# Layer 2's output projection as two blocks of seven products, with partial results and sums moved by accumulating transfers

## Chip, cores and metric

One core of one Trainium2 chip runs the whole program. The metric is the device time of one execution in microseconds; the kernel before has a median of 912.91 us over 3 runs (912.36 to 913.66). All data are float32.

## What is computed

Two layers over a 512 x 1024 sequence. Layer 1 is differential attention, layer 2 a spatial-gating MLP; each adds its result to the stream, and a final RMS norm ends the program. The change touches the end of layer 2:

```python
def spatial_gating_branch(h, w_in, v_gain, w_s, b_s):
    proj = h @ w_in                          # 512x1024 @ 1024x6144
    u = proj[..., :BRANCH]                   # BRANCH = 2048
    v = rms_norm(proj[..., BRANCH:2 * BRANCH], v_gain)
    gate = proj[..., 2 * BRANCH:]
    ...
    y = jnp.einsum('gts,bcsgd->bctgd', w, v) + b_s.T[:, :, None]
    return u * y * jax.nn.silu(gate)

x = x + y @ sgu_w_out[j]                     # 512x2048 @ 2048x1024
return rms_norm(x, final_norm)
```

## The kernel before

**Products in three terms.** A float32 product is made of three matmuls: each operand is split into a high part (ScalarE, ACT, a cast) and a low part (VectorE, DVE, the difference), and hi·hi, hi·lo and lo·hi are added in PSUM.

**Blocks of seven products.** Layer 2's input projection is cut into six blocks (n = 0 to 5), each 512 x 1024 by 1024 x 1024. `Quads` does a block by the Strassen-Winograd scheme: seven products of quarters instead of eight. It keeps the four quarters a, b, c, d of the weights in SBUF, loads each with two 512 KB transfers of SyncE's queue (SP, L355), and turns them step by step into the seven right operands: b-=d and a=b-a by DVE subtractions (L360, two of 128x1024 each), c+=a and a+=d by transfers of GpSimd's queue (POOL, L365) that add 1 MB within SBUF. Before each product a quarter is split, two pieces of 128x1024 by ACT (L373) and DVE (L374). `work(j)` yields these pieces for product j; `beside` sets one piece between two groups of matmuls, two products ahead of use. The left operands are quarters of the normed input and their sums s1 to s4, made once, since all six blocks have the same left side. A result quarter that several products share is held (`hold`, an ACT copy from PSUM to a tile "raw") and added later by DVE (`times`).

`product_n` (24 matmuls of 128x512) is used for blocks 0 and 1 (the values v), `product_t` (48 of 128x256) for blocks 2 to 5 (gates and u, transposed). `times` multiplies them into yT, 128 x 16 x 512, so that after block 3 the first half of y (yT 0 to 7) is complete, after block 5 the second.

**The end.** `out_half` runs twice, once for each half of the 1024 output columns: four chunks of y and weights, each split (ACT L267 and L129, DVE L268 and L130), 192 matmuls of 128x512 (L273 to L275) into four PSUM banks. After each half DVE adds the banks to the stream xr (L413), ACT squares it (L206) for the norm; after the second, `emit` forms the root by a chain of small DVE operations (L180 to L187), scales (ACT L1058, DVE L1059) and stores (SP L1061).

The engines issue in program order. A wait blocks everything behind it on the same engine. A scheduler orders the instructions of each engine from the order in which the program writes them.

Of the kernel before, what the change touches and what calls it, by code (L numbers as in the profile page):

```python
# [2 lines left out]

# [1 line left out]

# [45 lines left out]
def build(ctx, tc, x, rel_bias, attn_norm, w_in, lq1, lk1, lq2, lk2, subln, w_out,  # L51
# [14 lines left out]
    def bank(name):  # L66
        return psum.tile([P, S], F32, tag="ps", name=name)
# [5 lines left out]
    def wide_src(w, c, n0):  # L73
        return w[0, c * S:(c + 1) * S, n0:n0 + S].rearrange("(k p) n -> p k n", p=P), [4, S]
# [126 lines left out]
    def square(r, b, m=None):  # L201

        sl = slice(0, D) if m is None else slice(m * S, (m + 1) * S)
        c = 0 if m is None else m
        drop = yT[:, 10:12, :].rearrange("p k n -> p (k n)") if m is None else junk
        nc.scalar.activation(drop, xr[:, b, sl], AF.Square, accum_out=sq[r][b][:, c:c + 1])  # L206
        if c == 0:
            hv[r][b] = const.tile([P, 1], F32, name=f"hv{r}_{b}")

    def row_scale(r, b, halves):  # L210

        rs = small.tile([P, 1], F32, name="rs")
        if halves:
            nc.vector.scalar_tensor_tensor(hv[r][b], sq[r][b][:, 1:2], -0.5 / D, hv[r][b], ALU.mult, ALU.add)
        else:
            half_mean(r, b)
        newton(rs, hv[r][b], 1)
        return rs

    def half_mean(r, b):  # L220
        nc.vector.tensor_scalar(hv[r][b], sq[r][b][:, 0:1], -0.5 / D, -0.5 * EPS, ALU.mult, ALU.add)

    hi_last, hT_last, xs_last = [None], [None], [None]

# [102 lines left out]
    def temp():  # L327
        return wraw.tile([P, 2, S], F32, tag="raw", name="raw")
# [474 lines left out]
    quads = Quads(qp, [columns_of(sgu_w_in, n0) for n0 in columns])  # L803
# [49 lines left out]


    wst = sp.tile([P, KB, P], F32, name="wst")
    bs_bc = sp.tile([P, KB // 2 * P], F32, name="bs_bc")

    def spread_bias(m):
        src = sgu_b_s.rearrange("o g t -> o (g t)")[:, m * KB // 2 * P:(m + 1) * KB // 2 * P]
# [45 lines left out]
            nc.vector.tensor_tensor(v, of_bank(ps[i]), v, ALU.add)  # L905
            total(v, acc)

    i0 += 8
    assert i0 == sgu_at
    late = []  # L910
    for n in range(BR // D):
        for i in range(7):
# [86 lines left out]
            nc.vector.tensor_tensor(y, v.rearrange("p (j n) -> p j n", n=H), y, ALU.mult)  # L999

    VB = BR // D
    for m in range(2):
        for gates in (True, False):
            n = VB + 2 * m + (not gates)
            final = m == 1 and not gates
            t1 = temp()
            if final:
                t4, t2 = temp(), temp()
            for i in range(7):
                work = quads.work(7 * n + i + 2)  # L1010
                if final and i == 5:
                    limit[0] = len(chunks)
                    load(i0)
                if final and i > 4:
                    work = (split(i0, 2 * (i - 5) + h) for h in range(2))
                beside(product_t(py if i in (1, 3, 6) else px, sides[i], quads.forms[n, i], i in (0, 1, 3)), work)
                if m == 0 and gates and i in (2, 3):
                    for g in range(4 * i - 8, 4 * i - 4):
                        mix(g)
                    if i == 3:  # L1020
                        spread_bias(1)
                if m == 0 and not gates and i > 2:
                    mix(5 + i)
                if m == 1 and gates and i < 4:
                    mix(12 + i)
                if i == 0:
                    hold(t1, px)
                if i == (2 if m == 0 and gates else 1):
                    times(gates, m, 0, 0, py, t1)
                if i == 2:  # L1030
                    t2 = t2 if final else temp()
                    hold(t2, px)
                if i == 4:
                    t4 = t4 if final else temp()
# [9 lines left out]
    yps = tc.tile_pool(name="yp2", bufs=2)
    yp = yps.__enter__()
    fin = yp.tile([P, D], F32, name="fin", bufs=1)
    nc.scalar.dma_start(fin, final_norm.rearrange("(o d) -> o d", o=1).broadcast_to([P, D]))
    acc = [bank(f"acc{b}") for b in range(NB)]
# [3 lines left out]
    ov = out[0].rearrange("(b p) d -> p b d", p=P)
    acc = [bank(f"acc{b}") for b in range(NB)]
    last = residual(2, 1, acc)

    def emit(b):
        rs = row_scale(2, b, True)
        nc.scalar.activation(xr[:, b, 0:S], xr[:, b, 0:S], AF.Copy, scale=rs)  # L1058
        nc.vector.scalar_tensor_tensor(xr[:, b, S:D], xr[:, b, S:D], rs, fin[:, S:D], ALU.mult, ALU.mult)  # L1059
        for m in range(2):  # L1060
            nc.sync.dma_start(ov[:, b, m * S:(m + 1) * S], xr[:, b, m * S:(m + 1) * S])  # L1061

    def finish(b):
        add = last(b)
        if b < NB - 2:
            emit(b)
        elif b == NB - 1:
            emit(b - 1)
            with tc.issue_after(add.ins):
                emit(b)  # L1070
# [25 lines left out]
```

## Time and profile before

| | |
|---|---|
| median of 3 runs | 912.91 us |
| profiled execution, its own time | 909.98 us |
| its span, first to last instruction | 908.2 us |
| PE (TensorE matmul) busy | 885.3 us, 97% |
| DVE busy | 645.3 us, 71% |
| ACT busy | 476.9 us, 53% |
| granted TensorE clock | 0.997 of full speed |

The span is the part of the time that the engines' instructions cover. Busy time is a sum over all stages; what an engine is worth at the end of the program is read from the stretches of the end. In the profile a row "L374 DVE lo<-quarter,hi" is line 374 of the kernel, on DVE, writing the tile lo from quarter and hi; "[7.38 <-DMA quarter<-quarter]" behind a row says that its engine sat idle for 7.38 us before it and that a transfer ended that.

### The profile page before, as it was taken

What the parts mean: (1) busy time and instruction counts of PE and PEld (TensorE: products, weight loads), DVE (VectorE), ACT (ScalarE), POOL (GpSimd) and SP (SyncE); (2) the same over time, 40 slices, a digit from 0 to 9 for tenths busy, and PEclk for the clock granted to TensorE, in tenths of its full rate; (3) what the DMA queues carried; (4) which work ended last, traced back from release to release, by engine and by line L of the source; (5) the groups of instructions that cost most, each with busy time, mean ns of one, the idle gap of its engine ahead of it and who ended that gap; (6) DMA issues with size and microseconds to landing.
All of it is one profiled execution on the core that took longest, in us unless ns stands there. A gap on an engine that the chain in (4) does not pass through costs nothing.

```text
span 908.2 us, 14110 instructions
## 1 busy us (share of the span) xinstructions
PE 885.3 (97%) x5393; PEld 774.6 (85%) x5393; DVE 645.3 (71%) x1399; ACT 476.9 (53%) x1015; POOL 34.4 (4%) x52
## 2 busy tenths in 40 slices
PE   7999999999999999999999999998999999999996
PEld 5878999988888888888788887787999999998884
DVE  6945665447787788688886839857795878685634
ACT  7634555446565565566664526736453444454532
POOL 0000100000000000000000002000100000000000
PEclk9999999999999999999999999999999999999998
DMA  8637755373222332321312615554656464534202
GB/s 286 234 90 210 206 192 105 116 245 95 78 90 83 103 90 83 103 89 40 105 47 82 243 29 131 188 128 151 139 163 139 141 139 140 117 134 149 86 4 93
DMA packets 55828, 115.48 MB, mean 127 GB/s; under 512 B 3965, under 2 KB 20398, under 8 KB 52432
## 3 DMA queue, kind: packets, MB, share of 16 engines
q1 hardware_dynamic: 49120, 79.70, 26.5%
q0 software_dynamic: 5584, 33.56, 15.5%
q10 hardware_dynamic: 1056, 1.32, 0.4%
q8 instruction: 42, 0.69, 0.3%
q14 instruction: 26, 0.21, 0.1%
HBM read 89.36 MB, written 6.33 MB: 105 GB/s over the span
## 4 chain that ended last, share of the span: by engine, by line
PE 82%; DVE 10%; DMA 3%; ACT 3%; issue 1%; SPq 0%; ACTq 0%; DVEq 0%; POOLq 0%
PE px L319 15%; PE py L319 11%; PE psqk L254 6%; PE psqk L256 6%; PE psqk L255 6%; PE acc L273 5%; PE acc L275 5%; PE acc L274 5%; PE psv L480 5%; PE po L732 3%; PE pss L694 3%; DMA quarter<-quarter 2%; PE pa L721 2%; DVE lo L374 2%; PE psy L981 2%; PE px L307 1%
## 5 line engine op out<-in xcount | busy, mean ns | idle before, releaser
L374 DVE TENSOR_TENSOR lo<-quarter,hi 128x1024 fp32r<-128x1024 f32 x126 | 152.8, 1236 | 86.0 <-ACT hi L373 85.6
L373 ACT CAST hi<-quarter 128x1024 fp32r<-128x1024 f32 x126 | 128.9, 1047 | 125.7 <-DMA quarter<-quarter 45.7
L130 DVE TENSOR_TENSOR lo<-raw,hi 128x512 fp32r<-128x512 f32 x144 | 93.5, 687 | 39.4 <-ACT hi L129 39.3
L129 ACT CAST hi<-raw 128x512 fp32r<-128x512 f32 x144 | 81.8, 620 | 54.9 <-PE psqk L255 24.7
L254 PE MATMUL psqk<-hT,hi 128*128 128x512 f32 x256 | 101.7, 397 | 0.0
L256 PE MATMUL psqk<-hT,lo 128*128 128x512 f32 x256 | 99.9, 390 | 0.0
L255 PE MATMUL psqk<-hT,hi 128*128 128x512 f32 x256 | 99.9, 390 | 0.0
L707 ACT ACTIVATE e<-e,nm 128x384 f32<-128x384 f32 (+3 forms) x128 | 70.8, 554 | 47.7 <-DVE nm L704 47.3
L319 PE MATMUL py<-hT,hi 128*128 128x256 f32 x512 | 93.0, 284 | 0.0
L273 PE MATMUL acc<-hi,hT 128*128 128x512 f32 x224 | 88.2, 394 | 0.5 <-DVE on L666 0.5
L274 PE MATMUL acc<-lo,hT 128*128 128x512 f32 x224 | 87.3, 390 | 0.0
L275 PE MATMUL acc<-hi,hT 128*128 128x512 f32 x224 | 87.0, 390 | 0.0
L319 PEld LDWEIGHTS py<-hT,hi 128*128 128x128 f32 x512 | 79.8, 192 | 0.0
L319 PE MATMUL py<-hT,lo 128*128 128x256 f32 x256 | 72.5, 283 | 0.0
L704 DVE CUSTOM_DVE_ANT_0 e<-pss,bias 128x384 f32<-128x384 f32 (+3 forms) x128 | 57.3, 484 | 4.1 <-PE pss L694 3.9
L254 PEld LDWEIGHTS psqk<-hT,hi 128*128 128x128 f32 x256 | 48.1, 188 | 12.9 <-issue 2.6
L268 DVE TENSOR_TENSOR hT<-yT,hT 128x512 fp32r<-128x512 f32 x56 | 37.0, 690 | 29.8 <-PE acc L274 17.4
L256 PEld LDWEIGHTS psqk<-hT,lo 128*128 128x128 f32 x256 | 48.1, 188 | 10.1
L255 PEld LDWEIGHTS psqk<-hT,hi 128*128 128x128 f32 x256 | 48.1, 188 | 9.4
L267 ACT CAST hT<-yT 128x512 fp32r<-128x512 f32 x56 | 33.5, 621 | 41.1 <-PE acc L274 35.2
L360 DVE TENSOR_TENSOR quarter<-quarter 128x1024 f32<-128x1024 f32 x36 | 43.3, 1222 | 11.5 <-DMA quarter<-in_sgu_w_in 10.8
L273 PEld LDWEIGHTS acc<-hi,hT 128*128 128x128 f32 x224 | 42.1, 188 | 10.5 <-issue 1.6
(218 smaller groups left out, 2026.6 us busy)
## 6 DMA issues: line engine op xcount, KB each, us to landing
quarter<-in_sgu_w_in SPq DMA_DIRECT2D x48, 512.0 KB, 5.4
raw<-in_attn_w_in SPq DMA_DIRECT2D x38, 512.0 KB, 4.6
quarter<-quarter POOLq DMA_DIRECT2D x18, 1024.0 KB, 7.5
quarter<-in_attn_w_in SPq DMA_DIRECT2D x24, 512.0 KB, 4.8
raw<-in_attn_w_out SPq DMA_DIRECT2D x16, 512.0 KB, 4.4
raw<-in_sgu_w_out SPq DMA_DIRECT2D x16, 512.0 KB, 4.3
vd<-yT POOLq DMA_DIRECT2D x4, 1024.0 KB, 6.0
v<-vd POOLq DMA_DIRECT2D x4, 1024.0 KB, 5.1
```

The costliest lines, as they stand in the source:

```text
L129: nc.scalar.copy(hi[:, sl], raw)
L130: nc.vector.tensor_tensor(lo[:, sl], raw, hi[:, sl].bitcast(F32), ALU.subtract)
L254: nc.tensor.matmul(ps, lhsT=w.hi[:, k, cs], rhs=hT[0][:, k, :], start=(k == 0), stop=False)
L255: nc.tensor.matmul(ps, lhsT=w.hi[:, k, cs], rhs=hT[1][:, k, :], start=False, stop=False)
L256: nc.tensor.matmul(ps, lhsT=w.lo[:, k, cs], rhs=hT[0][:, k, :], start=False, stop=(k == KD - 1))
L273: nc.tensor.matmul(acc[b], lhsT=yh[:, j, bs], rhs=w.hi[:, j, :], start=(k == 0), stop=False)
L274: nc.tensor.matmul(acc[b], lhsT=yh[:, j, bs], rhs=w.lo[:, j, :], start=False, stop=False)
L275: nc.tensor.matmul(acc[b], lhsT=yl[:, j, bs], rhs=w.hi[:, j, :], start=False, stop=(k == KB - 1))
L319: nc.tensor.matmul(ps[f // 2][:, f % 2 * H:(f % 2 + 1) * H], lhsT=w[x][:, k, f * P:(f + 1) * P], rhs=a[y][:, k, :], start=clear, stop=(k = ...
L373: nc.scalar.copy(hi[:, sl], raw[:, sl])
L374: nc.vector.tensor_tensor(lo[:, sl], raw[:, sl], hi[:, sl].bitcast(F32), ALU.subtract)
L707: nc.scalar.activation(e[f][:, cs], e[f][:, cs], AF.Exp, scale=-1.0, bias=nm[:, col], accum_out=l[:, col])
```

## The change

The output projection becomes two more blocks of `Quads` (n = 6 and 7, kb = 0 and 1): the upper 1024 rows of the weights with yT 0 to 7, the lower 1024 with yT 8 to 15, each seven times `product_n`.

- The left operands are now quarters of y. Per block `left` makes s3 = y21 - y11 (DVE, L1017), y21 += y22 (transfer of POOL's queue, 512 KB, L1018), s2 = y11 - y21 (DVE, L1020), y12 += s2 (transfer, L1021), and splits seven operands (ACT L297, DVE L298, 128x1024 each). For block 6 that stands beside the products of block 5, for block 7 beside those of block 6.
- Of the results, each of products 0, 2 and 4 of a block is held by ACT (L331) and added to xr by a transfer of POOL's queue (`put_onto`, L1082, 512 KB, six in all); those of products 1, 3, 5 and 6 are added by DVE from PSUM (`onto`, L1078).
- Sixteen loads of 512 KB bring the weights by SP as quarters (L354) in place of sixteen as chunks.
- The final norm's scale of one column half and the squares are set beside the products of block 7 (`first_half`), the rest in `emit(b, m)`: rows 0 and 1 end after product 5, rows 2 and 3 after product 6.
- `fin` and `bs_bc` share one buffer, and `fin` is loaded at the end of block 5.

The core of the diff:

```diff
+    def rows_of(w, kb):
+        def of(name):
+            r, c = divmod("abcd".index(name), 2)
+            return wide_src(w, 2 * kb + r, c * S)[0]
+        return of
+
+    blocks = [columns_of(sgu_w_in, n0) for n0 in columns] + [rows_of(sgu_w_out, kb) for kb in range(2)]
+    quads = Quads(qp, blocks)
...
+    def left(kb, i):
+        y11, y12, y21, y22 = (quarter_of(kb, q, half) for half in range(2) for q in range(2))
+        if i == "s3":
+            s3[0] = temp().rearrange("p f n -> p (f n)").rearrange("p (k n) -> p k n", n=H)
+            nc.vector.tensor_tensor(s3[0], y21, y11, ALU.subtract)
+            nc.gpsimd.dma_start(y21, y22, accum_op=ALU.add)
+        elif i == "s2":
+            nc.vector.tensor_tensor(y11, y11, y21, ALU.subtract)
+            nc.gpsimd.dma_start(y12, y11, accum_op=ALU.add)
+        else:
+            part(*sides[i], (y11, y12, y11, s3[0], y21, y12, y22)[i])
+        yield
+    def left_work(kb, i):
+        for j in ([], [0], ["s3"], [1], [3, "s2"], [2], [4])[i]:
+            yield from left(kb, j)
+    def left_rest(kb, i):
+        for j in ([], [5], [6], [], [], [], [])[i]:
+            yield from left(kb, j)
...
                 work = quads.work(7 * n + i + 2)
-                if final and i == 5:
-                    limit[0] = len(chunks)
-                    load(i0)
-                if final and i > 4:
-                    work = (split(i0, 2 * (i - 5) + h) for h in range(2))
+                if n == OUT - 1:
+                    work = chain(work, left_work(0, i))
...
+    def onto(c, half, ps):
+        ms = slice(c * S, (c + 1) * S)
+        return [nc.vector.tensor_tensor(xr[:, b, ms], ps[b % 2], xr[:, b, ms], ALU.add)
+                for b in (2 * half, 2 * half + 1)]
+    def put_onto(c, half, t):
+        nc.gpsimd.dma_start(xr[:, 2 * half:2 * half + 2, c * S:(c + 1) * S], t, accum_op=ALU.add)
...
+    for kb in range(2):
+        n = OUT + kb
+        for i in range(7):
+            work = chain(quads.work(7 * n + i + 2), left_rest(kb, i), left_work(1, i) if kb == 0 else ())
+            beside(product_n(py if i in (1, 3, 6) else px, sides[i], quads.forms[n, i], i in (0, 1, 3)), work)
+            if i in (0, 2, 4):
+                t = temp()
+                hold(t, px)
+            if i == 1:
+                onto(0, 0, py)
+                put_onto(0, 0, t)
+            if i == 2:
+                put_onto(0, 1, t)
+            if i == 3:
+                onto(1, 1, py)
+            if i == 4:
+                put_onto(1, 1, t)
+                if kb:
+                    first_half(0, 0)
+            if i == 5:
+                onto(1, 0, px)
+                if kb:
+                    for b in range(2):
+                        emit(b, 1)
+                    first_half(1, 1)
+            if i == 6:
+                adds = onto(0, 1, py)
+                if kb:
+                    emit(2, 0)
+                    with tc.issue_after(adds[1].ins):
+                        emit(3, 0)
...
-    run(out_half(i0, 0, hT_store, range(4), acc, residual(2, 0, acc)))
...
-    run(out_half(i0 + 4, 1, hT_store, range(4), acc, finish))
```

**POOL, the last rows of its queue.** The name quarter is a quarter of the weights, yT is y, raw a held result, xr the stream. Before:

```order
L860 DMA bs_bc<-in_sgu_b_s 128x1024
L365 DMA quarter<-quarter 128x2048 x6
L1092 UNCONDITIONAL_BRANCH
```

and after the change:

```order
L866 DMA bs_bc<-in_sgu_b_s 128x1024
L364 DMA quarter<-quarter 128x2048 x6
L1018 DMA yT<-yT 128x4x256
L1021 DMA yT<-yT 128x4x256
L364 DMA quarter<-quarter 128x2048 x2
L1082 DMA xr<-raw 128x2x512
L1018 DMA yT<-yT 128x4x256
L1082 DMA xr<-raw 128x2x512
L1021 DMA yT<-yT 128x4x256
L1082 DMA xr<-raw 128x2x512
```

Behind block 5's two weight sums (the last two of the x6), which ended this queue, there now come 4 sums of y, 4 weight sums and 6 result sums (two weight sums and three result sums follow the rows shown).

**DVE, the middle of the output projection.** Before, near the end of its first half:

```order
L268 TENSOR_TENSOR hT_104<-yT,hT_103 128x512 x4
L130 TENSOR_TENSOR lo<-raw,hi 128x512 x3
L413 TENSOR_TENSOR xr<-acc_8041,xr 128x512
L130 TENSOR_TENSOR lo<-raw,hi 128x512
L221 TENSOR_SCALAR hv_0_8289<-sq_0_114 128x1
```

and after the change, beside block 6 (lo and hi are the parts of a weight quarter, hT parts of a y quarter, py a result):

```order
L1078 TENSOR_TENSOR xr<-py,xr 128x512 x2
L298 TENSOR_TENSOR hT_104<-yT,hT_103 128x4x256
L373 TENSOR_TENSOR lo<-quarter,hi 128x1024 x2
L1017 TENSOR_TENSOR raw<-yT 128x1024
L298 TENSOR_TENSOR hT_104<-yT,hT_103 128x4x256
L373 TENSOR_TENSOR lo<-quarter,hi 128x1024 x2
L1078 TENSOR_TENSOR xr<-py,xr 128x512
L1020 TENSOR_TENSOR yT<-yT 128x4x256
L1078 TENSOR_TENSOR xr<-py,xr 128x512
L298 TENSOR_TENSOR hT_104<-raw,hT_103 128x4x256
```

Splits of 128x512, which were ready long ahead of use, gave way to pieces of 128x1024 with the y differences among them; L1020 stands in DVE's row behind the transfer of L1018, which stands behind L1017, which stands behind the split of the quarter that the transfer a+=d has just summed.

## Rows read from the trace of the kernel before

**Rows 1.** Page, part 1: busy us (share of the span) and instructions.

```profile
PE 885.3 (97%) x5393; PEld 774.6 (85%) x5393; DVE 645.3 (71%) x1399; ACT 476.9 (53%) x1015; POOL 34.4 (4%) x52
```

**Rows 2.** Busy time by stretches: block 5, first part, rest and tail of the output projection.

```profile
core 0: us, PE busy (x) PEld busy (x) DVE busy (x) ACT busy (x) POOL busy (x), PEclk, DMA share, GB/s
772.40:812.40 40.00, 40.00 (x338) 40.00 (x337) 28.41 (x37) 20.26 (x30) 1.70 (x2) 1.00 0.46 119
812.40:850.00 37.60, 37.60 (x167) 31.14 (x167) 23.66 (x39) 19.15 (x35) 0.00 (x0) 1.00 0.42 136
850.00:899.60 49.60, 49.58 (x219) 40.77 (x217) 23.81 (x55) 16.69 (x34) 0.00 (x0) 1.00 0.10 35
899.60:908.20 8.60, 0.00 (x0) 0.00 (x0) 4.32 (x16) 2.06 (x4) 0.00 (x0) 0.72 0.49 184
```

**Rows 3.** Groups of instructions, 812.4 to 908: busy us, mean ns | idle before, releasers.

```profile
L273 PE MATMUL acc<-hi,hT 128*128 128x512 f32 x128 | 49.9, 390 | 0.0
...
L268 DVE TENSOR_TENSOR hT<-yT,hT 128x512 fp32r<-128x512 f32 x28 | 18.8, 691 | 23.4 <-PE acc L274 17.4 <-ACT hT L267 6.0
...
L129 ACT CAST hi<-raw 128x512 fp32r<-128x512 f32 x26 | 14.4, 617 | 2.5 <-DMA raw<-in_sgu_w_out 2.5
```

**Rows 4.** Timeline of PE, `product_n` of block 1: start us, us, engine, line, operation.

```profile
594.44 0.39 PE L307 MATMUL px<-hi,hT 128*128 128x512 f32 x1
...
599.20 0.39 PE L307 MATMUL px<-hi,hT 128*128 128x512 f32 x1
...
619.48 0.40 PE L307 MATMUL px<-hi,s1h 128*128 128x512 f32 x1
...
622.28 0.40 PE L307 MATMUL px<-hi,s1h 128*128 128x512 f32 x1
```

**Rows 5.** Timelines of DVE and ACT, block 5: operations back to back.

```profile
796.50 2.36 DVE L374 TENSOR_TENSOR lo<-quarter,hi 128x1024 fp32r<-128x1024 f32 x2 [0.18 <-ACT hi L373]
...
795.02 1.29 DVE L268 TENSOR_TENSOR hT<-yT,hT 128x512 fp32r<-128x512 f32 x2 [0.90 <-ACT hT L267]
...
790.38 1.05 ACT L373 CAST hi<-quarter 128x1024 fp32r<-128x1024 f32 x1
791.33 0.59 ACT L332 COPY raw<-px 128x512 f32<-128x512 f32 x1
```

**Rows 6.** Timelines around block 5's weight sums, by POOL, ACT and DVE.

```profile
772.40 0.85 POOL L365 DMA_DIRECT2D quarter<-quarter  x1 [35.24 <-DVE lo L374]
...
780.31 0.85 POOL L365 DMA_DIRECT2D quarter<-quarter  x1 [7.06 <-issue]
784.75 0.69 DVE L999 TENSOR_TENSOR yT<-raw,yT 128x512 f32<-128x512 f32 x1
...
788.00 2.00 ACT L373 CAST hi<-quarter 128x1024 fp32r<-128x1024 f32 x2 [7.38 <-DMA quarter<-quarter]
...
789.09 3.60 DVE L374 TENSOR_TENSOR lo<-quarter,hi 128x1024 fp32r<-128x1024 f32 x3 [3.65 <-ACT hi L373]
```

**Rows 7.** Weight sums (tile quarter, POOL): issue to landing in windows from 645, 693, 736, 780.

```profile
DMA to landing us min/median/max: 9.6/9.6/9.6
...
DMA to landing us min/median/max: 9.4/9.4/9.4
...
DMA to landing us min/median/max: 8.1/8.1/8.1
...
DMA to landing us min/median/max: 7.6/7.6/7.6
```

**Rows 8.** Timelines of POOL and SP: a+=d of blocks 3 and 4, and the loads behind.

```profile
693.29 0.85 POOL L365 DMA_DIRECT2D quarter<-quarter  x1 [7.32 <-DVE lo L374]
...
694.69 2.58 SPq L355 DMA_DIRECT2D quarter<-in_sgu_w_in  x2
...
736.31 0.85 POOL L365 DMA_DIRECT2D quarter<-quarter  x1 [6.62 <-DVE yT L984]
...
738.59 1.69 SPq L355 DMA_DIRECT2D quarter<-in_sgu_w_in  x2
```

**Rows 9.** Page, part 6, DMA issues: KB each, median us to landing.

```profile
quarter<-in_sgu_w_in SPq DMA_DIRECT2D x48, 512.0 KB, 5.4
...
quarter<-quarter POOLq DMA_DIRECT2D x18, 1024.0 KB, 7.5
```

**Rows 10.** Timeline of the tail.

```profile
899.20 0.39 PE L275 MATMUL acc<-hi,hT 128*128 128x512 f32 x1
...
900.33 0.68 DVE L413 TENSOR_TENSOR xr<-acc,xr 128x512 f32<-128x512 f32 x1
...
901.10 0.63 ACT L206 ACTIVATE junk<-xr 128x512 f32<-128x512 f32 x1 [1.61 <-DVE rs L187]
...
903.59 0.75 DVE L1059 SCALAR_TENSOR_TENSOR xr<-xr,rs,fin 128x512 f32<-128x512 f32 x1
```

More of the change, by code (lines that the diff above doesn't have):

```diff
@@ L2 @@
 from contextlib import ExitStack
+from itertools import chain
 import numpy as np
@@ L206, in square, with row_scale @@
         nc.scalar.activation(drop, xr[:, b, sl], AF.Square, accum_out=sq[r][b][:, c:c + 1])
-        if c == 0:
+        if b not in hv[r]:
             hv[r][b] = const.tile([P, 1], F32, name=f"hv{r}_{b}")
-    def row_scale(r, b, halves):
+    def row_scale(r, b, halves, second=1):
         rs = small.tile([P, 1], F32, name="rs")
         if halves:
-            nc.vector.scalar_tensor_tensor(hv[r][b], sq[r][b][:, 1:2], -0.5 / D, hv[r][b], ALU.mult, ALU.add)
+            nc.vector.scalar_tensor_tensor(hv[r][b], sq[r][b][:, second:second + 1], -0.5 / D, hv[r][b], ALU.mult,
+                                           ALU.add)
         else:
@@ L218, in row_scale, with half_mean @@
         return rs
-    def half_mean(r, b):
-        nc.vector.tensor_scalar(hv[r][b], sq[r][b][:, 0:1], -0.5 / D, -0.5 * EPS, ALU.mult, ALU.add)
+    def half_mean(r, b, m=0):
+        nc.vector.tensor_scalar(hv[r][b], sq[r][b][:, m:m + 1], -0.5 / D, -0.5 * EPS, ALU.mult, ALU.add)
     hi_last, hT_last, xs_last = [None], [None], [None]
@@ L855, in build @@
     wst = sp.tile([P, KB, P], F32, name="wst")
-    bs_bc = sp.tile([P, KB // 2 * P], F32, name="bs_bc")
+    bs_bc = sp.tile([P, KB // 2 * P], F32, tag="row", name="bs_bc")
     def spread_bias(m):
@@ L1001, in build, with quarter_of @@
     VB = BR // D
+    OUT = 3 * VB
+    def quarter_of(kb, q, half):
+        return yT[:, 8 * kb + 4 * q:8 * kb + 4 * q + 4, half * H:(half + 1) * H]
+    def left(kb, i):
[10 more added lines that the diff above has]
+        yield
+    s3 = [None]
+    def left_work(kb, i):
[4 more added lines that the diff above has]
+            yield from left(kb, j)
     for m in range(2):
@@ L1030, in build @@
                 if i == 2:
-                    t2 = t2 if final else temp()
+                    t2 = temp()
                     hold(t2, px)
                 if i == 4:
-                    t4 = t4 if final else temp()
+                    t4 = temp()
                     hold(t4, px)
@@ L1040, in build @@
                     times(gates, m, 0, 1, py, t2)
+    fin = sp.tile([P, D], F32, tag="row", name="fin")
+    nc.scalar.dma_start(fin, final_norm.rearrange("(o d) -> o d", o=1).broadcast_to([P, D]))
+    ov = out[0].rearrange("(b p) d -> p b d", p=P)
+    def onto(c, half, ps):
[4 more added lines that the diff above has]
+        nc.gpsimd.dma_start(xr[:, 2 * half:2 * half + 2, c * S:(c + 1) * S], t, accum_op=ALU.add)
@@ new lines, in first_half, with emit @@
+    def first_half(m, half):
+        ms = slice(m * S, (m + 1) * S)
+        for b in (2 * half, 2 * half + 1):
+            square(2, b, m)
+            half_mean(2, b, m)
+            nc.vector.tensor_tensor(xr[:, b, ms], xr[:, b, ms], fin[:, ms], ALU.mult)
+    def emit(b, m):
+        square(2, b, m)
+        rs = row_scale(2, b, True, m)
+        o, n = slice((1 - m) * S, (2 - m) * S), slice(m * S, (m + 1) * S)
+        nc.scalar.activation(xr[:, b, o], xr[:, b, o], AF.Copy, scale=rs)
+        nc.vector.scalar_tensor_tensor(xr[:, b, n], xr[:, b, n], rs, fin[:, n], ALU.mult, ALU.mult)
+        for sl in (o, n):
+            nc.sync.dma_start(ov[:, b, sl], xr[:, b, sl])
@@ L1041, in build @@
     scope.__exit__(None, None, None)
     quarters.__exit__(None, None, None)
[L1044 to L1048, printed above, removed]
-    run(out_half(i0, 0, hT_store, range(4), acc, residual(2, 0, acc)))
-    for b in range(NB):
-        nc.vector.tensor_tensor(xr[:, b, 0:S], xr[:, b, 0:S], fin[:, 0:S], ALU.mult)
@@ L1052, in build @@
[L1052 to L1070, printed above, removed]
```

11 lines of the change are left out of this document (1 added, 10 removed).

## Prediction

> **What bounds the kernel now.** I read the page first: PE is busy for 97% of the span [rows 1], so time can only be won by taking matmuls out or by filling its few gaps. The stretches say where: in block 5 and in the output projection PE is busy for the whole of the time, to the last hundredth, and only the tail of 8.6 us is without it [rows 2]. The groups of the output projection agree: its matmuls waited 0.0 us, while DVE sat idle for 23.4 us before L268 alone, with PE as the releaser [rows 3]. So the rate of PE sets the end there, and the reader is to see how much room the others have: DVE 24 of 50 us between 850 and 899.6, but 28.4 of 40 in block 5 [rows 2]. The granted clock is 1.00 in all these stretches, the upper level (2.4 GHz); it falls only in the tail, where PE has nothing to do, and I price nothing for it.
>
> **The gain on PE.** 384 matmuls took 87.2 us, 812.4 to 899.6 [rows 2], 0.227 each. Now there are 2 x 7 x 24 = 336, in the form of `product_n`. Its price depends on the left operand: with hT, 21 matmuls lie between the two first rows of group 4, 4.76 / 21 = 0.2267 us; with s1, 12 lie between the two others, 2.80 / 12 = 0.2333 [rows 4]. Per block four products read hT (s3 among them), three read s1, s2 and s4. That makes 5.44 us for eight products and 5.60 for six: 43.5 + 33.6 = 77.1 us. **Gain 10.1 us**, if PE never waits. The block then ends at 889.5.
>
> **What DVE has to do now.** Two of its 128x1024 pieces back to back take 2.36 us, one alone 1.22, so the pitch is 1.14; 128x512 has 0.60 (1.29 less 0.69) [rows 5]. Block 5 gets 18 pieces of weights, 7 of y sums and splits and 14 of `times`: 25 x 1.14 + 14 x 0.60 = 36.9 of 40 us. Block 6 gets 18 and 9 and 8: 35.6 of 38.6 us. The room that blocks before had is gone: each wait of DVE is now nearly a wait of PE. ACT gets 14 casts for 14 of DVE's splits at 1.05 and is under that. The row that matters is therefore DVE's own order, and what it waits for in it.
>
> **The chain through it.** In block 5 the sum a+=d is issued at 780.31 and has landed at 788.00, when ACT's cast begins [rows 6]. DVE idled for 3.65 us up to 789.09 for it. The first y sum (L1018) stands behind a+=d in POOL's queue. What 512 KB cost there no row shows. Moved beside the one ahead it would add nothing, with the whole price of 1 MB 7.5 us [rows 9]; I take 3, a little under half, since its start is hidden behind the transfer ahead. So it lands at L = 790.9, and there DVE stands, at L1020. From L on, DVE's order has 18 pieces of 128x1024 and 7 of 128x512 up to the last subtraction of block 6's a: 18 x 1.14 + 7 x 0.60 = 24.7 us. Only then may c+=a go, and behind its landing a+=d, 7.6 us each [rows 7] and 0.1 for the hand-over: L + 40.1. The lo split behind it (a cast of 1.05, two pieces of 1.14) and s3 (1.22) end at L + 44.7. The second y sum stands alone: half of 7.5 at the least, all of it at most [rows 9]; I take 5.0, near the plain load's 5.4 [rows 9]. Then L1020 (1.2), ACT's cast of s2 (1.05) and behind it the copy of the held result (0.6) [rows 5], which frees the bank that product 5 of block 6 writes: **L + 52.5 = 843.4**. With PE packed that product would begin at 812.4 + 3 x 5.44 + 2 x 5.60 = 839.9. **Stall 3.5 us.**
>
> **What else is added.** Behind that PE is packed again, but for the copies of products 2 and 4 of block 7: ahead of them on ACT stand two squares of `first_half` and casts. One square has 0.63 us [rows 10]; between 0 and 3, I take **1.2**. In the **tail** the last matmul begins at 899.20, the last addition at 900.33 and the last scaling at 903.59 [rows 10]. Now two additions end it and not one (0.60 more) and two rows share the chain of squares and roots (some 0.8 to 1.4 more, by one square and the small operations): **1.6**. The results that transfers add (six of 512 KB, and two y sums of L1021) lie behind PE's work and nobody waits within a product's time; I cost them at nothing: their cover is a product of 5.4 us before DVE's next addition. The 16 loads by SP replace 16 of the same size; `fin` is in place long before its use. Without any contention the sum is -10.1 + 3.5 + 1.2 + 1.6 = -3.8 us.
>
> **Contention.** Block 5's a+=d had only one late load beside it. Now SP loads block 6's a behind it, as in the blocks before. In those the same sum took 9.6, 9.4 and 8.1 us against 7.6 [rows 7]: 0.5 to 2.0 more. The 9.4 had its load 1.4 us behind, the 8.1 one 2.3 us [rows 8]; after the change it will be some 1.7 us behind, and I take 1.0, once for block 5 (L later) and once for block 6. The second y sum meets a load too: nothing to 2.5 (the difference between 5.0 and the whole of 7.5), taken 0.5, half of the 1.0 for half the bytes. **Together 2.5.** The sum is -3.8 + 2.5 = **-1.3 us**. The profiled execution would go from 909.98 to 908.7; the median shown lies 2.9 above that execution, so I forecast 912.91 - 1.3 = **911.6**. A difference under 0.2% (1.8 us) could hardly be measured; the forecast is within it.
>
> The Trainium skill (DMA: Bandwidth & Descriptors, "Anatomy of one DMA — SWDGE (gpsimd) path") puts a transfer at 2.0 us plus its bytes over 436 KB per us, so 4.4 us for 1 MB and 3.2 for 512 KB. By it, an estimate, the chain would be 2 x 3.2 + 1.8 = 8.2 us shorter, no stall would be left, and the change would win as the first rival below says. The trace disagrees for these transfers, which read both sides and add: a median of 7.5 us [rows 9]. The same page ("Issuing engines are not separate DMA queues") says that transfers of all issuing engines interleave on the same 16 DMA engines. That speaks against "nobody stands behind them", and the trace agrees: 8.1 to 9.6 us with loads behind, 7.6 without [rows 7].
>
> **The rivals.** (1) *The queues keep up.* If the y sums are as cheap as half the bytes and DVE's row slides ahead by some 4 us (an order with fewer waits than I count), the stall at 843 goes: -10.1 + 1.2 + 1.6 = -7.3, **905.6**. For it: PE has two banks and work is made two products ahead. Against: 35 to 37 us of DVE in 39 to 40. (2) *The y sums are paid by the piece, slower.* A quarter of the weights is one run of 2048 numbers in each partition, a quarter of y is four runs of 256. If a transfer's price follows its runs rather than its bytes, 512 KB cost at least the 7.5 of 1 MB: 4.5 more at the first L1018 and 2.5 more at the second. DVE stands in front of both, and every us goes to PE: -1.3 + 7.0 = +5.7, **918.6**. It decides from some 3 us above my two prices on: then slower by more than 0.2%. For it: no transfer of POOL's in the trace adds such short runs; against: DMA is busy for 0.46 of block 5 only [rows 2]. (3) *The change doesn't do what it says:* DVE stands behind L1018, and ACT behind DVE; that is in the forecast already.
>
> **How the numbers follow.** Forecast 0.53, its own range -3.8 to +2.7 (contention 0 to 2.0 + 2.0 + 2.5), 909.1 to 915.6; rival 1 0.27; rival 2 0.20. Faster by over 0.2%: all of rival 1 and about a third of the forecast, 0.46; within: 0.24; slower: rival 2 and the rest, 0.30. The range takes in rival 1's value and nearly rival 2's: 905.3 to 918.0.
>
> **What would show it.** PE's matmuls fall by 48, and its busy time by about 10 us. DVE's L1020 shows idle time with the transfer yT as its releaser, twice; the first L1018 lands near 791 to 792, the second 5 to 6 us after its issue. PE waits some 4 to 6 us for px or for the split of an operand near product 5 of block 6, little before and behind; the tail is about 10 us long. I am wrong if block 5 itself stalls for more than 2 us, if the largest wait of PE lies in block 7, or if PE waits for nothing at all.

## The result, and the profile after

| | before | after |
|---|---|---|
| median | 913.83 us (6 runs) | 919.33 us (6 runs) |
| ratio to before, 95% interval | | 1.0069 [1.0051, 1.0086] |
| profiled execution: time, span | 909.98, 908.2 us | 920.77, 919.0 us |
| PE busy | 885.3 us, 97% | 883.3 us, 96% |
| granted TensorE clock | 0.997 | 0.990 |

The change is slower by 6.3 us (0.0069 of 912.9); the forecast was 1.3 faster, and its range ended at 918.0. The profiled execution of after is its slowest run. Of its 10.8 us of longer span 2.8 lie ahead of block 5, whose first matmul starts that much later than before (half of them in the first 180 us, which the change does not touch), so stretches are compared from there on. The stretches of after, cut at the first matmul of blocks 5, 6 and 7 and at the end of the last product (they answer to [rows 2]):

```profile
core 0: us, PE busy (x) PEld busy (x) DVE busy (x) ACT busy (x) POOL busy (x), PEclk, DMA share, GB/s
775.10:820.10 45.00, 42.05 (x338) 41.64 (x338) 32.56 (x36) 23.78 (x28) 4.33 (x4) 0.96 0.66 164
820.10:870.90 50.80, 43.68 (x171) 34.58 (x170) 40.34 (x41) 23.36 (x27) 8.00 (x7) 0.90 0.77 176
870.90:909.30 38.40, 38.40 (x169) 31.42 (x168) 27.90 (x49) 19.46 (x32) 5.34 (x5) 1.00 0.55 110
909.30:919.00 9.70, 0.41 (x2) 0.00 (x0) 5.25 (x21) 2.89 (x6) 0.00 (x0) 0.76 0.44 163
```

Block 7 is the forecast: 38.4 us with PE busy for all of it, against 4 x 5.44 + 3 x 5.60 = 38.6. Block 5 takes 45.0 us where it took 40.0 before, block 6 takes 50.8 where packed products take 38.6. So 17.2 us of stops eat the gain of 10. Two things are in them, idle time (2.95 and 7.1 us, the stretch less PE's busy time) and a lower clock (0.96 and 0.90).

Who holds PE up is read from its waits between 640 and 919 (engine, line, waited for: us, times, longest), which before had none there:

```profile
PE px L306 <- ACT raw L331: 6.2, 2, 3.4
PE px L318 <- DVE lo L373: 2.5, 1, 2.5
PE px L318 <- ACT raw L331: 1.3, 2, 0.9
PE py L306 <- DVE raw L998: 0.9, 1, 0.9
```

And who holds those up, from the timelines of POOL, ACT and DVE (the rows of before are [rows 6]):

```profile
784.55 0.86 POOL L364 DMA_DIRECT2D quarter<-quarter  x1 [6.81 <-issue]
785.19 1.54 POOL L1018 DMA_DIRECT2D yT<-yT  x1
...
825.44 0.89 POOL L364 DMA_DIRECT2D quarter<-quarter  x1 [19.92 <-ACT hi L372]
834.76 0.86 POOL L364 DMA_DIRECT2D quarter<-quarter  x1 [8.43 <-DVE lo L373]
...
849.58 1.30 POOL L1018 DMA_DIRECT2D yT<-yT  x1 [11.38 <-DVE raw L1017]
...
795.21 2.00 ACT L372 CAST hi<-quarter 128x1024 fp32r<-128x1024 f32 x2 [10.79 <-DMA quarter<-quarter]
...
844.32 1.99 ACT L372 CAST hi<-quarter 128x1024 fp32r<-128x1024 f32 x2 [11.03 <-DMA quarter<-quarter]
...
798.69 1.23 DVE L1020 TENSOR_TENSOR yT<-yT 128x1024 f32<-128x1024 f32 x1 [10.90 <-DMA yT<-yT]
...
800.43 2.35 DVE L373 TENSOR_TENSOR lo<-quarter,hi 128x1024 fp32r<-128x1024 f32 x2
...
855.46 1.22 DVE L1020 TENSOR_TENSOR yT<-yT 128x1024 f32<-128x1024 f32 x1 [2.56 <-DMA yT<-yT]
```

DVE stands 10.90 us at L1020 in block 5. The low part of block 5's a+=d, the right operand of product 4, is made behind it (800.43) although ACT had its high part from 795.21 on: that is block 5's stop. In block 6 a+=d is issued at 834.76, 14.6 us after the block's start; block 5 of before had it at 8.0 us.

### The profile page after: what moved, and what is told of

Its sections match the earlier page's. It is cut to its first block, busy times and chain, and to the rows that moved or that the text cites. A ratio compares the mean times of both kernels' runs of the same rounds, so it can differ in the third digit from the quotient of the medians.

```text
span 919.0 us, 14029 instructions
## 1 busy us (share of the span) xinstructions
PE 883.3 (96%) x5345; PEld 770.5 (84%) x5345; DVE 669.4 (73%) x1397; ACT 488.2 (53%) x1005; POOL 50.6 (6%) x66
## 5 line engine op out<-in xcount | busy, mean ns | idle before, releaser
L373 DVE TENSOR_TENSOR lo<-quarter,hi 128x1024 fp32r<-128x1024 f32 x154 | 185.8, 1233 | 95.5 <-ACT hi L372 95.1
L372 ACT CAST hi<-quarter 128x1024 fp32r<-128x1024 f32 x154 | 157.3, 1048 | 164.6 <-DMA quarter<-quarter 74.0
L128 DVE TENSOR_TENSOR lo<-raw,hi 128x512 fp32r<-128x512 f32 x112 | 72.9, 687 | 38.1 <-ACT hi L127 38.1
L127 ACT CAST hi<-raw 128x512 fp32r<-128x512 f32 x112 | 64.0, 621 | 48.1 <-PE psqk L254 24.7
L359 DVE TENSOR_TENSOR quarter<-quarter 128x1024 f32<-128x1024 f32 x44 | 52.9, 1220 | 15.4 <-DMA quarter<-in_sgu_w_in 11.8
L318 PEld LDWEIGHTS py<-hT,lo 128*128 128x128 f32 x256 | 49.1, 192 | 0.0
L306 PE MATMUL py<-hi,hT 128*128 128x512 f32 x112 | 44.1, 394 | 1.5 <-DVE raw L998 0.9
L308 PE MATMUL py<-hi,hT 128*128 128x512 f32 x112 | 43.9, 392 | 0.0
L307 PE MATMUL py<-lo,hT 128*128 128x512 f32 x112 | 43.6, 390 | 0.0
L479 PE MATMUL psv<-hi,hT 128*128 128x512 f32 x128 | 42.0, 408 | 1.6 <-ACT hT L240 1.6
L364 POOL DMA_DIRECT2D quarter<-quarter x22 | 19.6, 890 | 406.3 <-DVE lo L373 230.4
```

The lines of the kernel that those rows point to most:

```text
L127: nc.scalar.copy(hi[:, sl], raw)
L128: nc.vector.tensor_tensor(lo[:, sl], raw, hi[:, sl].bitcast(F32), ALU.subtract)
L306: nc.tensor.matmul(ps[i], lhsT=a[0][:, k, rs], rhs=w[0][:, k, :], start=(start and k == 0), stop=False, **more)
L307: nc.tensor.matmul(ps[i], lhsT=a[0][:, k, rs], rhs=w[1][:, k, :], start=False, stop=False, **more)
L308: last_mm[:] = [nc.tensor.matmul(ps[i], lhsT=a[1][:, k, rs], rhs=w[0][:, k, :], start=False, stop=(k == 3), **more)]
L318: nc.tensor.matmul(ps[f // 2][:, f % 2 * H:(f % 2 + 1) * H], lhsT=w[x][:, k, f * P:(f + 1) * P], rhs=a[y][:, k, :], start=clear, stop=(k = ...
```

## Experiments

Theories: **A**, DVE stands at L1020 with its row behind it, and with DVE full nothing is caught up. **B**, SP's loads slow the weight sums a+=d. **C**, a y sum is paid by its short runs. **D**, the lower clock behind a stop costs time of its own. **E**, DVE has no room at all. Stretches are cut at block starts, in us; the ratio is to the kernel before, run beside it.

| kernel | block 4 | block 5 | block 6 | block 7 | tail | ratio [95%] |
|---|---|---|---|---|---|---|
| before | 43.7 | 40.0 | 87.2 for both | | 8.6 | 1 |
| the change | | 45.0 | 50.8 | 38.4 | 9.7 | 1.0069 [1.0051, 1.0086] |
| y0_early | 52.7 | 40.1 | 45.2 | | | 1.0054 [1.0034, 1.0074] |
| y1_early | | 46.5 | 47.8 | | | 1.0069 [1.0050, 1.0087] |
| y01_early | 54.9 | 40.1 | 43.4 | | | 1.0054 [1.0035, 1.0073] |
| fill | | 52.2 | 51.8 | | | 1.0187 [1.0166, 1.0209] |
| y0_sum_ahead | | 40.1 | 49.1 | 38.3 | 9.5 | 1.0012 [0.9997, 1.0026] |
| y01_sum_ahead | | 40.1 | 46.3 | 40.2 | 9.3 | 1.0012 [1.0000, 1.0024] |
| y_dve | | 40.1 | 46.5 | 39.2 | 9.6 | 0.9985 [0.9968, 1.0001] |
| res_dve | | 44.7 | 45.6 | 42.4 | | 1.0063 [1.0048, 1.0078] |
| load_behind5 | | 45.4 | 52.0 | | | 1.0068 [1.0043, 1.0092] |
| run_of_4k | | 42.2 | 51.3 | 38.4 | 9.5 | 1.0066 [1.0041, 1.0091] |
| mix | | 40.1 | 43.4 | 40.2 | 9.6 | **0.9953** [0.9933, 0.9972] |
| mix_fill | | 40.1 | 43.3 | | | 0.9941 [0.9919, 0.9963] |
| mix_load_behind | | 40.1 | 42.2 | 39.9 | | **0.9941** [0.9919, 0.9964] |

### The sums of y earlier in the program

```diff
+                if n == OUT - 2 and i in (3, 6):
+                    work = chain(work, left(0, "s3" if i == 3 else "s2"))
...
+            work = chain(left(1, "s3") if (kb, i) == (0, 0) else (), quads.work(7 * n + i + 2), left_rest(kb, i),
```

The first hunk is y0_early, the last y1_early, both are y01_early, with a buffer of its own for s3; in left_work's lists s3 leaves its old place, and s2 of block 7 moves one product ahead. In y0_early and y01_early s2 and s4 of block 6 overwrite two quarters of y before these are split, so two left operands are not the layer's; the work is the same. Expected of y0_early, y1_early, y01_early:

> The sums of y for block 6 (L1017, L1018, L1020, L1021) are made beside block 4 and not beside block 5. Theory A (DVE stands behind the transfer L1018, and everything behind DVE slides by that wait): the 10.9 us of idle DVE at 787 to 799 go, block 5's stall of PE falls from 5.0 us to under 1.5, block 6's c+=a is issued some 7 us sooner, the stall before product 4 of block 6 goes; only the second L1018's stall is left (3 us idle and the slow clock behind it). Time 8 to 12 us less than the change's 919.3: 907 to 911. Theory B (the sum a+=d of block 5 is slowed by SP's loads, and that alone delays PE): a+=d still lands 10 us after its issue, block 5 still stalls 2 to 4 us, and the gain is 3 to 5 us: 914 to 916. Theory C (the price of the y sums by the piece, rival 2): gain of some 4.5 us, and the transfers themselves take 7 us or more.

> Only the sums of y for block 7 move: s3 and its transfer stand ahead of block 6's a+=d in DVE's and POOL's order, s2 one product sooner. Theory A: L1020 of block 7 no longer waits (2.6 us of idle DVE), the last stop of PE (855.4 to 858.3, and the clock at its lower level for some 3 us behind it) goes, 3 to 5 us less; but a+=d lands up to 3 us later, since the y sum is ahead of it in the queue: net 0 to 4 us less than 919.3. Theory B: 0 to 2 us less. Theory C: a+=d lands some 7 us later, and the kernel is 2 to 4 us slower than the change.

> Both moves together. Theory A: the stalls of blocks 5 and 6 fall from 17 us to under 4, time 903 to 908, faster than the kernel before by 0.6 to 1.1%. Theory B: 912 to 915. Theory C: 910 to 914.

Measured: 1.4 us less than the change for y0_early (0.0015 of 912.9) where theory A promised 8 to 12, nothing for y1_early (A: 0 to 4), and for y01_early no more than for y0_early: theory A missed twice. But the stop did not vanish, it moved. Block 5 is clean (40.1 us) and block 4 has 9.0 us more than before. DVE and POOL of y0_early in block 4:

```profile
738.02 1.54 POOL L1018 DMA_DIRECT2D yT<-yT  x1
...
752.12 1.23 DVE L1020 TENSOR_TENSOR yT<-yT 128x1024 f32<-128x1024 f32 x1 [12.25 <-DMA yT<-yT]
```

The scheduler had put L1020, written three products later, close behind the transfer again, and DVE stood there 12.25 us. So the place in the program's text had not settled the place in DVE's row; y0_sum_ahead, below, settles it by a dependence.

### Matmuls that nobody reads

```diff
+    def fill(n, i, count):
+        w = quads.forms[n, i][0]
+        for _ in range(count):
+            nc.tensor.matmul(psy[3], lhsT=w[:, 0, 0:P], rhs=w[:, 0, :], start=True, stop=True)
```

> The change with 13 matmuls of 128x512 that nobody reads (into a free PSUM bank, after product 3 of block 5 and products 3 and 4 of block 6), so that PE is busy while it waits: some 2.95 us in each of three stops of 3 us. Theory D (the lower clock behind each stop costs 6 us by itself): PE's rows keep 1.00, and the time falls by 4 to 6 us. Theory A (PE's stops are set by the chain DVE, POOL, ACT, and most of the slow clock is hidden behind it; only what follows the last stop counts): 0 to 2 us less.

Measured: 1.0187, 10.8 us slower than the change (0.0118 of 912.9), which none of the theories had. With the fill the scheduler set DVE's row otherwise: two subtractions L359, which wait for a load (4.92 us), stand ahead of splits, and the load behind them came late in turn. This tells nothing on the clock; mix_fill, below, repeats it where the row ahead of the stop is the same.

### The transfer away from L1020, and no transfer

y0_sum_ahead makes only s3 and the first transfer beside block 4; L1020 waits for block 5's first splits anyway and stays there. y01_sum_ahead adds y1_early's edit for s3. y_dve replaces the transfers of y (L1018, and L1021 alike), res_dve those of the results; the hunks of y0_sum_ahead, y_dve and res_dve in this order:

```diff
+                if (n, i) == (OUT - 2, 3):
+                    work = chain(work, left(0, "s3"))
...
-            nc.gpsimd.dma_start(y21, y22, accum_op=ALU.add)
+            nc.vector.tensor_tensor(y21, y21, y22, ALU.add)
...
-        nc.gpsimd.dma_start(xr[:, 2 * half:2 * half + 2, c * S:(c + 1) * S], t, accum_op=ALU.add)
+        x = xr[:, 2 * half:2 * half + 2, c * S:(c + 1) * S]
+        nc.vector.tensor_tensor(x, x, t, ALU.add)
```

> Only s3 and the first transfer of y for block 6 (L1017, L1018) stand beside block 4, with a buffer of their own for s3; L1020 and L1021 stay where they are beside block 5, so that DVE comes to L1020 long after the transfer has landed. Theory A (what costs is that DVE stands at L1020, with its whole row behind it): no idle time before L1020 in block 5, block 5 takes 40 to 41.5 us and not 45, block 6's weight sums are issued 5 us sooner after the block's start; ratio to the kernel before 0.997 to 1.002, where the change has 1.0069. Theory B (the weight sum a+=d is late by itself, because SP's loads share its way): a+=d of block 5 still lands 10 us after its issue, block 5 still takes 43 to 45 us; ratio 1.004 to 1.007.

> The same, and block 7's s3 and transfer ahead of block 6's a+=d as well. Theory A: no wait of DVE for a y sum is left in either block; ratio 0.994 to 1.000. Theory B: as y0_sum_ahead or up to 2 us slower, since block 6's a+=d stands behind one more transfer.

> The y sums by four DVE additions of 128x1024 in the places of the four transfers (L1018, L1021): 2.3 us more of DVE in each of two blocks and no transfer to wait for. Theory A: the 13.5 us that DVE stood at L1020 become 4.6 us of work; block 5 takes 41 to 43 us, block 6 44 to 46 in place of 51; ratio 0.998 to 1.003. Theory B: ACT still waits some 30 us for the weight sums, ratio 1.004 to 1.007. Theory E (DVE has no room: more work on it is as bad as a wait): 1.007 or more.

> The six held results are added to xr by DVE (128x1024 each, from SBUF) and not by transfers. Theory A: nobody waited long for those transfers, and DVE gets 3.4 us more in each of blocks 6 and 7, whose row is full: 0 to 4 us slower than the change, ratio 1.007 to 1.011. Theory B (the transfers stand in each other's way): the second L1021 and block 7's weight sums land 2 to 4 us sooner; ratio 1.003 to 1.006.

Measured: 1.0012 and 0.9985, 5.2 and 7.7 us less than the change (0.0057 and 0.0084 of 912.9), in theory A's ranges (block 6 of y_dve, 46.5 us, just above its 44 to 46), and against B and E: DVE of y_dve does 3.6 us more in block 5 than the change's (36.14 against 32.56) and PE never waits. Blocks 5 and 6 of y_dve:

```profile
772.20:812.30 40.10, 40.10 (x338) 40.10 (x338) 36.14 (x39) 23.67 (x28) 1.71 (x2) 1.00 0.59 158
812.30:858.80 46.50, 41.88 (x171) 33.49 (x170) 37.19 (x38) 23.13 (x27) 5.30 (x5) 0.93 0.72 169
```

y01_sum_ahead gave no more in the time, outside A's range (0.994 to 1.000): it took 2.8 us out of block 6 and put 1.9 into block 7. res_dve is the change within the intervals, at the edge of what A and B expected, so its time decides nothing between them: block 6 gains 5.2 us, block 7 loses 4.0. The gain of block 6 is not the transfers' alone, for the scheduler also set the second L1020 later in DVE's row (854.39, without a wait). The second y sum itself took as long without a result transfer beside it: 6.1 us to its first reader (846.01 to 852.09, ACT's cast) against 5.9 in the change. So the trace gives no sign that the result transfers cost. A stop of 8 us in block 6 is left in y_dve, and that is no y sum. Its rows:

```profile
814.82 0.86 POOL L364 DMA_DIRECT2D quarter<-quarter  x1 [33.81 <-ACT hi L372]
824.58 0.86 POOL L364 DMA_DIRECT2D quarter<-quarter  x1 [8.90 <-DMA quarter<-quarter]
...
835.20 1.99 ACT L372 CAST hi<-quarter 128x1024 fp32r<-128x1024 f32 x2 [10.96 <-DMA quarter<-quarter]
...
836.28 2.36 DVE L373 TENSOR_TENSOR lo<-quarter,hi 128x1024 fp32r<-128x1024 f32 x2 [9.31 <-ACT hi L372]
838.56 1.22 DVE L1017 TENSOR_TENSOR raw<-yT 128x1024 f32<-128x1024 f32 x1
...
844.83 1.22 DVE L1020 TENSOR_TENSOR yT<-yT 128x1024 f32<-128x1024 f32 x1
```

The two weight sums take 9.1 and 10.5 us from issue to landing, and DVE idles 9.31 us with the y sums of block 7, which need no weights, waiting behind the split in its row.

### Both, and the loads

mix makes block 6's first y sum by a transfer beside block 4, block 7's by DVE, and all of block 7's y operations but the last sum ahead of the split that waits for a+=d. late_a, y_dve_late_a and mix_late_a move SP's load of the next quarter a (the last hunk; in blocks 5 and 6 for the first, in block 6 for the two others):

```diff
+            ahead = {0: ["s3"], 2: [1, "s2"]}.get(i, []) if kb == 0 else []
+            work = chain(*(left(1, j) for j in ahead), quads.work(7 * n + i + 2), left_rest(kb, i),
...
-            if i == 3:
+            if i == 3 and n not in (5, 6):
                 self.load(n + 1, "a", s["b"])
             if i == 4:
+                if n in (5, 6):
+                    self.load(n + 1, "a", s["b"])
```

> The change with one thing moved: SP's load of the next block's quarter a (two of 512 KB) is issued one step later in blocks 5 and 6, behind the split that waits for a+=d, so that it no longer shares its way with a+=d and the first y sum; the order on every engine but SP is the same. Theory B (SP's loads slow these transfers): a+=d of block 5 lands 7.6 to 8.5 us after its issue and not 10.6, the first L1018 some 3 us sooner, a+=d of block 6 8 us and not 9.5; time 3 to 5 us less than the change, ratio 1.002 to 1.004. Theory A alone (the place of L1020 in DVE's row, whatever the loads do): a+=d as before, ratio 1.006 to 1.008.

> y_dve with the load of block 7's quarter a one step later. Theory B: block 6's a+=d lands 7.6 to 8.5 us after its issue and not 10.5, PE's stop before product 4 of block 6 shrinks by 2 to 3 us; ratio 0.994 to 0.997 against 0.9985 of y_dve. If the load is then late for block 7: PE waits there, and the ratio is 0.998 or more.

> Block 6's first y sum by a transfer beside block 4 (as y0_sum_ahead), block 7's two y sums by DVE, and these ahead of the split that waits for block 6's a+=d, in the time when y_dve's DVE stood idle (9.3 us). Theory A: block 5 has 2.3 us less of DVE than y_dve, block 6's sums start sooner, and behind a+=d DVE has four pieces less before product 5: block 6 takes 42 to 44 us (46.5 in y_dve, 50.8 in the change), ratio 0.992 to 0.996. Theory B alone: a+=d stays as late as in y_dve and the ratio stays at 0.998.

> mix, and block 7's quarter a loaded one step later. Theories A and B together: block 6 takes 40 to 42 us; ratio 0.990 to 0.994. A alone: as mix.

Measured: mix 0.9953 [0.9933, 0.9972], **faster than both kernels**: 4.3 us less than before, 10.6 less than the change. Block 6 took 43.4 us, as theory A had said (42 to 44). late_a had 1.0069 [1.0044, 1.0095], y_dve_late_a 0.9990 [0.9974, 1.0006], mix_late_a 0.9953 [0.9935, 0.9971]: each as without the edit, but this speaks neither for nor against B. SP issues a load as soon as its buffer is free, wherever the text has it. Timelines of late_a's POOL and SP:

```profile
783.94 0.86 POOL L364 DMA_DIRECT2D quarter<-quarter  x1 [6.81 <-issue]
...
784.14 0.88 SPq L354 DMA_DIRECT2D quarter<-in_sgu_w_out  x2
```

The load goes 0.20 us behind a+=d, in the change 0.21. So in load_behind5 and mix_load_behind ACT issues it, in the order of ACT's casts (`nc.scalar.dma_start`; the rows of DVE and POOL are as without the edit); mix_fill is mix with the fill from above behind product 3 of block 6; run_of_4k replaces the first sum of block 6's y by one of the same bytes in one run per partition (that sum of y is left out, so the output is not the layer's):

```diff
+            if kb:
                 nc.gpsimd.dma_start(y21, y22, accum_op=ALU.add)
+            else:
+                nc.gpsimd.dma_start(s3[0].rearrange("p k n -> p (k n)"), wst[:, 0:8, :].rearrange("p g t -> p (g t)"),
+                                    accum_op=ALU.add)
```

> The change with the load of block 6's quarter a issued by ACT, behind its casts that wait for block 5's a+=d (late_a did not move that load: SP issues it as soon as its buffer is free). Rows of DVE and POOL are in the same order. Theory B (the load that SP issues within 0.2 us of a+=d slows it): a+=d lands 7.6 to 8.2 us after its issue and not 10.6, the y sum behind it 11.5 to 13 us after that issue and not 14.1; DVE's wait at L1020 is 2 us shorter, ratio 1.004 to 1.006. If the load is without weight: 10.6 and 14.1 again, ratio 1.007.

> The change with the first L1018 (y21 += y22, four runs of 1 KB in each partition) replaced by a sum of the same 512 KB in one run of 4 KB in each partition, for which L1020 then waits; the sum of y is left out, so the output is not the layer's. Theory C (price by the run): the transfer lands 2.5 to 3.5 us after a+=d has, and both are done 11.5 to 12.5 us after a+=d's issue where the change needs 14.1; PE's stop in block 5 is 2 us shorter. Price by the byte: 14 us again.

> mix with the load of block 7's quarter a issued by ACT behind the casts that wait for block 6's a+=d. Theory B: that sum lands 7.6 to 8.5 us after its issue (10.2 in mix), PE's stop of 3.0 us before product 4 of block 6 falls under 1 us and the slow clock behind it goes; block 6 takes 39 to 41 us (43.4 in mix); ratio 0.991 to 0.993, if the load is not then late for block 7. If the load is without weight: as mix, 0.995.

> mix with 13 matmuls that nobody reads, in the one stop that is left before product 4 of block 6 (2.95 us of work for 3.0 us of stop). Theory D (the lower clock behind a stop costs time of its own where nothing waits behind it): PE's granted clock stays 1.00 in block 6, products 4 and 5 take 11.2 us and not 12.8, the time falls by 1 to 2 us; ratio 0.993 to 0.9945. Theory A: same time, 0.995.

DVE and ACT of load_behind5, where a+=d is issued at 782.41 and the load 1.74 us behind it:

```profile
790.95 2.00 ACT L372 CAST hi<-quarter 128x1024 fp32r<-128x1024 f32 x2 [7.15 <-DMA quarter<-quarter]
...
797.38 1.22 DVE L1022 TENSOR_TENSOR yT<-yT 128x1024 f32<-128x1024 f32 x1 [10.20 <-DMA yT<-yT]
```

a+=d is ready 8.5 us after its issue, and not 10.7 (795.21 less 784.55). But the y sum (L1022 in this kernel is L1020) is no sooner: 15.0 us after that issue where the change has 14.1. The load shares the way with one or the other, and DVE waits for the later. So B holds for a+=d alone and not for the time.

res_dve shows the same without an edit to the load. The order of its DVE and ACT is the change's up to block 6, but its load (the first of the three that SP's row merges) goes 1.69 us behind a+=d:

```profile
780.80 0.86 POOL L364 DMA_DIRECT2D quarter<-quarter  x1 [6.84 <-issue]
...
782.49 17.67 SPq L354 DMA_DIRECT2D quarter<-in_sgu_w_out  x3
...
789.35 2.00 ACT L372 CAST hi<-quarter 128x1024 fp32r<-128x1024 f32 x2 [7.20 <-DMA quarter<-quarter]
...
795.66 1.23 DVE L1020 TENSOR_TENSOR yT<-yT 128x1024 f32<-128x1024 f32 x1 [10.14 <-DMA yT<-yT]
...
797.41 2.35 DVE L373 TENSOR_TENSOR lo<-quarter,hi 128x1024 fp32r<-128x1024 f32 x2
```

a+=d is ready after 8.6 us and the y sum after 14.9. This also parts theory A from a late a+=d: a+=d is ready 16.6 us after the start of block 5 (772.8), in y0_sum_ahead 16.0, and yet block 5 takes 44.7 us and not 40.1. What is left is the place of L1020: the split could begin behind the first of the two casts, at 790.4, and begins at 797.41.

run_of_4k, a+=d issued at 782.30, the load 1.70 us behind it (784.00):

```profile
789.82 2.00 ACT L372 CAST hi<-quarter 128x1024 fp32r<-128x1024 f32 x2 [6.15 <-DMA quarter<-quarter]
...
794.47 1.23 DVE L1024 TENSOR_TENSOR yT<-yT,raw 128x1024 f32<-128x1024 f32 x1 [7.44 <-DMA raw<-wst]
```

Both are done after 12.2 us, in the range of theory C, and block 5 takes 42.2 us. The fair comparison is with the runs whose load goes at the same moment, res_dve (14.9) and load_behind5 (15.0), and not with the change: some 2.7 us of the y sum's price are its short runs. The time is unchanged (1.0066): block 6 stops 0.5 us more, and what remains of the gain is within the interval.

mix_load_behind moved half of the load only: the first of its two transfers went out 0.02 us behind a+=d, the second behind the cast. a+=d was ready after 9.2 us (10.3 in mix), and block 6 takes 42.2 us, 1.2 less than mix; the intervals of the two overlap, so this gain is shown by the trace alone. mix_fill: the granted clock (last but two) in mix and, behind it, in mix_fill, with the 13 extra matmuls in the stop:

```profile
835.00:837.00 2.00, 0.00 (x0) 1.00 1.13 218
837.00:839.00 2.00, 1.10 (x3) 0.71 0.23 40
839.00:841.00 2.00, 2.00 (x6) 0.50 0.30 49
```

```profile
835.00:837.00 2.00, 2.00 (x10) 1.00 1.13 227
837.00:839.00 2.00, 1.94 (x9) 1.00 0.39 70
839.00:841.00 2.00, 1.79 (x8) 1.00 0.16 26
```

The clock stays at its upper level, and block 6 takes 43.3 us in place of 43.4. The slow matmuls of mix cost 1.6 us; in their place PE of mix_fill meets three waits that mix did not have, for a split (0.2 us idle), for ACT's copy of a held result (0.3) and for a DVE addition (0.3), which from matmul start to matmul start take 1.5 us. So theory D does not hold in this stop. Where no wait follows, the lower level is on the path: behind the last stop of the change, at 858.3, seven matmuls of its chain of waits, from the first row to the second, take 0.43 us each and not 0.23, and with those at the edges 1.6 us go:

```profile
860.08 0.43 PE px L306
...
862.64 0.43 PE px L306
```

## Why the prediction was wrong

**The gain on PE** was right: packed blocks take 38.3 to 38.4 us in the change and y0_sum_ahead, 38.6 forecast. **The tail** (9.7 us, forecast 8.6 + 1.6 = 10.2) was near. The 1.2 us in block 7 did not come.

**The chain** was the right mechanism, and in the places named: L1020 waits twice for yT, product 5 of block 6 begins behind it, and PE is packed from there on. Its terms were mis-sized, nearly all to one side. From the start of block 5 on, forecast and measured:

| step | forecast | measured | late by |
|---|---|---|---|
| block 5's start to the issue of a+=d | 8.0 | 9.5 | 1.5 |
| to DVE's start at L1020 | 7.6 + 3 + 1.0 = 11.6 | 14.1 | 2.5 |
| to the issue of block 6's c+=a | 24.7 | 26.8 | 2.0 |
| to that of its a+=d | 7.7 | 9.3 | 1.6 |
| to ACT's cast of it | 7.7 + 1.0 = 8.7 | 9.6 | 0.9 |
| to the issue of the second L1018 | 4.6 | 5.3 | 0.7 |
| to DVE's second L1020 | 5.0 + 0.5 = 5.5 | 5.9 | 0.4 |
| to product 5 of block 6 (858.30) | 2.85 | 2.84 | 0.0 |

The first row is no price of the change: block 4's a+=d took 9.9 us in this execution and 8.0 in res_dve, and what stands behind it slid; in res_dve block 5's a+=d is issued 8.0 us after the block's start, as forecast.

The rows make 9.6 us; 0.2 more up to the end of the last product (1.6 of lower clock for the 1.2 in block 7 that did not come) and 0.5 less in the tail leave 9.3, from a forecast of -1.3 to the +8.0 that this execution lost from block 5 on (143.9 us against 135.9 before). **The step that failed** is the price of the first y sum behind a+=d, "I take 3, a little under half, since its start is hidden". In the change's execution the load goes 0.21 us behind a+=d and not 1.7, so that a+=d took 10.7 us and the y sum 3.5 more, 14.1 together against 11.6. res_dve has the load where the prediction put it, and there a+=d took 8.6 us, as forecast (7.6 + 1.0), and the y sum 6.3 more and not 3. y_dve, without the y sum and with the load 1.70 us behind, has its a+=d ready in 8.2 us (780.16 to 788.36). So a y sum behind a+=d costs 5.9 us in the change and 6.7 in res_dve, about twice the 3. The next largest term, the 25 operations up to c+=a, took 26.8 us: 1.31 of the 2.0 too much is a wait of DVE for a load among them.

**Block 5** was named as what would make the forecast wrong, if it stopped for more than 2 us; it took 5 us too long. The order of DVE showed the reason and the prediction passed it by: the split of a+=d stands behind L1020 (798.69 and 800.43 in the rows above), so product 4 of block 5 waits for the y sum too. The prediction's chain counts these pieces only as work on the way to block 6's c+=a. y0_sum_ahead, where the transfer stands beside block 4 and L1020 waits for nothing, wins back 4.9 us in block 5 and 5.2 in the time.

**The rivals.** Rival 1 (the queues keep up) fell. Rival 2 ended at nearly the measured time, 918.6, in part by luck: short runs are paid, some 2.7 us in the first y sum (run_of_4k), which cost 5.9 to 6.7 us where the rival had 7.5, but the second cost 5.9 and not 7.5, and the rest came from the other steps. Rival 3 held as the text said: DVE stands behind L1018. The rule of the Trainium skill (DMA: Bandwidth & Descriptors, "Issuing engines are not separate DMA queues") that transfers of all engines interleave on the same DMA engines agrees with the change and load_behind5: the pair of sums was done after 14.1 us with the load at once and after 15.0 with it 1.74 us behind, with a+=d ready after 10.7 and 8.5.

**What stays open:** why block 6's c+=a takes 9.1 us in y_dve, where block 5's took 6.9. Nearly all its bytes had moved at 821.0 us, but it landed only at 823.9; in block 5 they had moved at 778.5 and it landed at 779.4. What fills those 2.9 us no run shows. Open is also what block 6's a+=d would take with the whole of its load behind it. The fair test of the clock was made in one stop only.

## What to carry to other kernels

A transfer that replaces an engine's work takes no load off that engine if the engine's own next instruction waits for it: look in the engine's order, not in the program's text, for the first reader of what the transfer writes, and for what stands behind that reader. If the reader cannot stand far behind by a dependence, the plain addition is cheaper: 1.14 us of DVE against a wait of 10.90. Price a chain of transfers by rows in which the same queue and the same neighbours are busy: besides the first, six of the eight steps of this chain came out 0.4 to 2.5 us longer than priced, and none came out shorter.

## What the runs showed of the hardware

A 1 MB sum within SBUF, with a 512 KB sum 0.6 us behind it, was ready after 10.7 to 11.0 us where a load went out 0.2 us behind it (the change, late_a, y1_early, fill) and after 8.5 to 8.6 where it went out 1.7 us behind (load_behind5, res_dve). The pair was done after 14.1 to 14.4 and 14.9 to 15.0 us, so the load's moment chose which of them paid and moved the end by less than 1 us. And PE kept busy with matmuls that nobody reads held its clock at the upper level through a stop of 3 us, which changed the block by 0.1 us.
